# Weight splitting in a two-layer hybrid decoder kernel: half-chunk splits shared by VectorE and GpSimd, against whole-chunk splits on VectorE alone

## The chip, the cores and the metric

The kernel runs on one core of one Trainium2 chip. The time is device microseconds (us) of one execution; before the change it is 1144.73 us, the median of three runs (1144.65 to 1145.38). The engines are called as the profile calls them: PE is the matrix engine (TensorE) and PEld its weight loads, DVE is VectorE, ACT is ScalarE, POOL is GpSimd, and SP is the engine whose queue issues the DMA transfers here. Each engine works through its own list of instructions in order, so an instruction that waits holds all that stand behind it on that engine.

## The reference

Two layers act on x of 256 tokens by 2048 features, in float32. `c` is one vector of 2048, the same for all tokens. In each layer:

```python
shift, scale, gate = jnp.split(silu(c) @ w_ada[l] + b_ada[l], 3, axis=-1)     # w_ada[l]: 2048 x 6144
h = rms_norm(x, norm_w[l]) * (1.0 + scale) + shift
parts = jnp.split(h @ w_in[l], bounds, axis=-1)          # w_in[l]: 2048 x 7704
# three groups of heads read these parts: gated linear attention, gated delta rule, differential attention
y = jnp.concatenate([o_gla, o_gdn, o_diff], axis=-1) @ w_out[l]               # w_out[l]: 2048 x 2048
x = x + gate * y
```

The first line is called the modulation, `h` the modulated input, and the three groups of heads the mixers.

## The kernel before

**Weights.** All large products run on PE with operands of type float32r. To keep float32's accuracy, each operand is split into two parts whose sum is exact, and three products are formed: high by high, high by low and low by high. The modulated input is split into `hh` and `hl` by `modulate`. The weights come from memory in chunks of up to 1024 columns on 128 partitions (512 KB) into one of six buffers `raw`. `weights` (L302) splits each chunk in pieces of 512 or 536 columns: ACT's cast (L316) writes the high part `wh`, and a subtraction of it from `raw` (L319) writes the low part `wl`. Of each seven pieces POOL makes the low part of three and DVE of four. `wh` and `wl` have five buffers of 536 columns each.

**The modulation** has 48 rows of 128 features per layer, in twelve groups of four. Each group needs eight transfers of 1024 columns (`rawa`, from the same six buffers as `raw`); DVE multiplies each by a row of silu(c) and sums along the row in the same instruction (L338), which gives two half sums per feature. When the eighth is done, four or fewer small DVE instructions (L343 to L351) add the halves, the bias, and for the scale the 1 and the norm weight, into `ada`. Groups 0 to 7 give scale and shift for two k tiles each, groups 8 to 11 give the gate. With a k tile's `ada`, `modulate` makes `hn` on DVE (L402), `hh` on ACT (L403) and `hl` on DVE (L404). The function `advance` spreads the groups over the input projection's steps: all twelve of layer 0 and three of layer 1 are done within layer 0.

**Order.** The input projection goes over blocks of output columns and ranges of k tiles (`STEPS`); a block's sums over its range are kept in PSUM (`pt`, `pf`) and are copied out by ACT the first time (L448) and added by DVE later (L450). The mixers are Python generators which are resumed between pieces of the projections, so that their instructions stand between those of the projections on every engine. A scheduler sets each engine's final order by priority and its own estimate; the splits, the modulation's products and the copies from PSUM have a raised priority (`AHEAD`), and the mixers a higher one. The output projection (`py`) follows in three steps and adds into `xr` on DVE (L1200).

**Transfers.** All weights are issued from SP's one queue, `raw` at L308 and `rawa` at L333, in one order. An issue waits there until its buffer has been released by the last reader of what was in it: the low part's subtraction for `raw`, the product for `rawa`.

Of the kernel before, what the change touches and what calls it, by code (L numbers as in the profile page):

```python
# [18 lines left out]
P = 128  # L19
# [3 lines left out]
L = 2  # L23
# [30 lines left out]
# Blocks of columns in the order in which they are computed.  # L54
# [11 lines left out]
# The steps of each layer's input projection: blocks b0..b1-1 over k tiles k0..k1-1. (Layer 0's modulation arrives k tile  # L66
# by k tile, and layer 1's follows the norm.)
# [4 lines left out]
# The k tiles of the output projection's steps: gated linear attention, delta rule, differential attention.  # L72
# [3 lines left out]
def in_chunks(layer, i):  # L76
    """Chunks of w_in for one step: lists of (block, k0, k1) that share one transfer."""
# [23 lines left out]
def _chunk_pieces(chunk):  # L101
    """Sizes of the pieces, of whole k tiles, in which a chunk is split into two parts."""
    out = [0]
    for b, a, z in chunk:
        for _ in range(a, z):
            if out[-1] + _width(b) > 536:
                out.append(0)
            out[-1] += _width(b)
    return out


# Column layout of the packed per-partition parameters.
# [17 lines left out]
def _constants():  # L130
# [6 lines left out]
    # Of each chunk of 64 tokens, its own columns alone.  # L137
# [14 lines left out]
def hybrid_trunk(ctx: ExitStack, tc: tile.TileContext, x, cvec, pos, par, w_ada, w_in, w_out, w_lr, qkn, adt, cst, out):  # L152
# [7 lines left out]
    wsp = ctx.enter_context(tc.tile_pool(name="wsp", bufs=5))  # L160
# [8 lines left out]
    def reg(i, name):  # L169
        """One of the work tiles that the mixers hand on to each other, in the order of the program."""  # L170
        return work.tile([P, 512], F32, name=name, tag=f"R{i}", bufs=1)
# [12 lines left out]
    # The mixers are generators, resumed between pieces of the projections; they yield the tensor engine's time after which  # L184
    # their next step's inputs are expected, or a condition. PSUM banks and work tiles are handed on in this order.
# [905 lines left out]
    for l in range(L):  # L1091
# [132 lines left out]
        if l == 0:  # L1224
            sq = [temp("sqs", T, 1)]
# [81 lines left out]
```

## Time and profile before

| | before |
|---|---|
| median of three runs | 1144.73 us |
| span of the profiled execution, first to last instruction | 1140.7 us |
| busy: PE, DVE, ACT, POOL | 1060.2, 913.4, 613.7, 619.9 us |
| weight pieces split | 620: low part of 354 on DVE, of 266 on POOL |
| products of the modulation (L338) | 192: 184 from `rawa`, 8 from the first tiles `fr` |
| DMA | 273.31 MB, 240 GB/s over the span |

The profile is of one execution. Busy time is the time in which an engine had an instruction running; PE's ends are modelled. In the views by line, a row gives the engine, the operation, the tile written and the tiles read, the shapes and the count, then the busy time and the mean duration of one, and then the idle time just before these instructions with what ended it. The chain of waits is followed back from the last instruction to what released each step. "Issue" in it is time in which an engine waited for nothing that the profile shows.

### The profile page before, as it was taken

How to read it: one execution, taken by the hardware profiler on the slowest of the kernel's cores; microseconds unless marked ns; L12 is line 12 of the kernel's file. 1: busy time of each engine (PE TensorE's matmuls, PEld its weight loads, DVE VectorE, ACT ScalarE, POOL GpSimd, SP SyncE). 2: the span in 40 equal slices, each digit the busy share in tenths (PEclk: the TensorE clock that was granted, in tenths of full speed). 3: DMA queues.
4: the chain of work that ended last, by engine and by line, in shares of the span. 5: the costliest groups of instructions: out<-in, count | busy, mean ns of one | idle time of the engine just before them, and what ended most of it. 6: DMA issues, size and time to landing. Idle time of an engine off the chain costs nothing.

```text
span 1140.7 us, 20595 instructions
## 1 busy us (share of the span) xinstructions
PE 1060.2 (93%) x7398; PEld 927.9 (81%) x7398; DVE 913.4 (80%) x1484; ACT 613.7 (54%) x1367; POOL 619.9 (54%) x550
## 2 busy tenths in 40 slices
PE   4989998889799999999988999998899999999998
PEld 3769876678788886898986877888799877879998
DVE  6899999998999759799788796767656877767853
ACT  4645434445654474666535545476454556557642
POOL 5444444456474586666753554366443666644642
PEclk9999999999999998999998999999899999999999
DMA  9888988888777454666689889785435555667462
GB/s 356 300 291 315 332 292 305 273 290 286 266 258 256 150 166 166 238 206 194 197 283 341 326 313 326 251 310 185 149 99 178 190 183 185 224 219 252 138 201 95
DMA packets 76807, 273.31 MB, mean 240 GB/s; under 512 B 8816, under 2 KB 9888, under 8 KB 76576
## 3 DMA queue, kind: packets, MB, share of 16 engines
q1 hardware_dynamic: 76704, 271.99, 69.8%
q8 instruction: 58, 0.95, 0.3%
q14 instruction: 45, 0.37, 0.1%
HBM read 267.76 MB, written 4.19 MB: 238 GB/s over the span
## 4 chain that ended last, share of the span: by engine, by line
PE 45%; DVE 25%; DMA 11%; issue 9%; POOL 5%; ACT 3%; SPq 0%; DVEq 0%; ACTq 0%; POOLq 0%
PE pt L191 21%; PE py L191 9%; DVE rawa L338 7%; DVE wl L319 7%; DMA rawa<-in_w_ada 7%; PE pf L191 6%; DMA raw<-in_w_in 4%; POOL wl L319 3%; DVE on_gdn L673 2%; PE Z_ps L191 1%; ACT wh L316 1%; PE o_gdn L191 1%; DVE z L450 1%; PE o_gla L191 1%; DVE hn L402 1%
## 5 line engine op out<-in xcount | busy, mean ns | idle before, releaser
L319 POOL TENSOR_TENSOR wl<-raw,wh 128x512 fp32r<-128x512 f32 (+2 forms) x266 | 403.8, 1532 | 355.8 <-ACT wh L316 319.1
L316 ACT CAST wh<-raw 128x512 fp32r<-128x512 f32 (+2 forms) x620 | 367.3, 613 | 311.2 <-PE pt L191 122.6
L338 DVE SCALAR_TENSOR_TENSOR rawa<-rawa,c_row 128x1024 f32<-128x1024 f32 x184 | 262.5, 1431 | 84.3 <-DMA rawa<-in_w_ada 73.0
L319 DVE TENSOR_TENSOR wl<-raw,wh 128x512 fp32r<-128x512 f32 (+2 forms) x354 | 285.5, 821 | 52.1 <-ACT wh L316 50.9
L191 PE MATMUL pt<-wl,hh 128*128 128x512 f32 (+1 forms) x768 | 294.1, 385 | 16.7 <-DVE wl L319 12.7
L191 PE MATMUL pt<-wh,hl 128*128 128x512 f32 (+1 forms) x768 | 289.2, 381 | 1.0 <-DVE hl L404 0.9
L191 PE MATMUL pt<-wh,hh 128*128 128x512 f32 (+1 forms) x768 | 257.4, 383 | 8.5 <-ACT hh L403 6.9
L191 PEld LDWEIGHTS pt<-wl,hh 128*128 128x128 f32 x768 | 146.3, 191 | 52.8 <-DVE wl L319 20.0
L191 PEld LDWEIGHTS pt<-wh,hh 128*128 128x128 f32 x768 | 144.5, 190 | 41.2 <-ACT hh L403 9.1
L191 PEld LDWEIGHTS pt<-wh,hl 128*128 128x128 f32 x768 | 145.8, 190 | 29.6 <-DVE hl L404 2.5
L191 PE MATMUL pf<-hh,wl 128*128 128x256 f32 x512 | 148.8, 292 | 6.4 <-POOL wl L319 4.0
L191 PE MATMUL pf<-hh,wh 128*128 128x256 f32 x512 | 148.2, 290 | 0.0
L191 PE MATMUL pf<-hl,wh 128*128 128x256 f32 x512 | 147.6, 289 | 0.0
L191 PEld LDWEIGHTS pf<-hh,wl 128*128 128x128 f32 x512 | 99.0, 194 | 9.5 <-POOL wl L319 4.9
L191 PEld LDWEIGHTS pf<-hh,wh 128*128 128x128 f32 x512 | 99.4, 194 | 2.3 <-issue 1.2
L191 PEld LDWEIGHTS pf<-hl,wh 128*128 128x128 f32 x512 | 99.1, 194 | 1.1 <-issue 0.7
L191 PE MATMUL py<-ogg,wh 128*128 128x256 f32 x512 | 99.4, 289 | 0.0
L191 PE MATMUL py<-odf,wh 128*128 128x256 f32 x512 | 91.6, 281 | 0.8 <-ACT odf L1044 0.7
L191 PEld LDWEIGHTS py<-ogg,wh 128*128 128x128 f32 x512 | 80.5, 189 | 0.9 <-issue 0.2
L191 PEld LDWEIGHTS py<-odf,wh 128*128 128x128 f32 x512 | 78.4, 188 | 1.5 <-ACT odf L1044 0.9
L191 PE MATMUL py<-odf,wl 128*128 128x256 f32 x256 | 72.0, 282 | 2.6 <-POOL wl L319 1.3
L191 PE MATMUL py<-ogg,wl 128*128 128x256 f32 x256 | 73.1, 287 | 0.0
(279 smaller groups left out, 1416.7 us busy)
## 6 DMA issues: line engine op xcount, KB each, us to landing
raw<-in_w_in SPq DMA_DIRECT2D x224, 512.0 KB, 4.6
rawa<-in_w_ada SPq DMA_DIRECT2D x184, 512.0 KB, 4.7
raw<-in_w_out SPq DMA_DIRECT2D x64, 512.0 KB, 4.2
raw<-in_w_in SPq DMA_DIRECT2D x20, 402.0 KB, 4.1
fr<-in_w_ada SPq DMA_DIRECT2D x8, 512.0 KB, 9.9
xt<-in_x SPq DMA_DIRECT2D x4, 512.0 KB, 5.3
xr<-in_x SPq DMA_DIRECT2D x4, 512.0 KB, 7.8
xs<-xr SPq DMA_DIRECT2D x1, 2048.0 KB, 11.7
```

The lines of the kernel that those rows point to most:

```text
L191: return PE.matmul(o, lhsT=lhsT, rhs=rhs, start=start, stop=stop, **kw)
L316: ACT.copy(wh, r)
L319: e.tensor_tensor(wl, r, wh.bitcast(F32), ALU.subtract)
L338: DVE.scalar_tensor_tensor(raw, raw, 1.0, cb, ALU.mult, ALU.mult, accum_out=sums[:, i:i + 1])
L402: DVE.scalar_tensor_tensor(h, rb, scale, xt[:, i, :], ALU.mult, ALU.mult)
L450: DVE.tensor_tensor(d, src, d, ALU.add)
L673: DVE.scalar_tensor_tensor(yi[:, s:T], src[:, 0:T - s], pcol("conv", w + 3 - s), yi[:, s:T], ALU.mult, ALU.add)
```

## The change

It has three parts.

1. `weights` no longer cuts a chunk into pieces. One ACT cast writes the high part of the whole chunk and one DVE subtraction the low part; POOL has none. `wh` and `wl` now have three buffers of 1024 columns each instead of five of 536. The mixers are still polled after every 536 columns or fewer.
2. The small DVE instructions at the end of a modulation group go. At the start of the program DVE halves the biases and multiplies the norm weights in (three instructions). Then one ACT instruction per feature adds the two half sums, with scale and bias, through its accumulator. There are 96 of these, four per group; each can run when its own feature's two products are done.
3. To make room, `junk` (a discarded output) shrinks from 512 to 256 columns, and `sqs` uses the work tile R9.

```diff
-    wsp = ctx.enter_context(tc.tile_pool(name="wsp", bufs=5))
+    wsp = ctx.enter_context(tc.tile_pool(name="wsp", bufs=3))
...
-    def weights(src, sizes):
-        n = sum(sizes)
-        raw = wraw.tile([P, RAW], F32, name="raw", tag="raw")
+    def weights(src, n):
+        raw = wraw.tile([P, RAW], F32, name="raw", tag="raw")[:, 0:n]
+        wh = wsp.tile([P, RAW], F32R, name="wh", tag="wh")[:, 0:n]
+        wl = wsp.tile([P, RAW], F32R, name="wl", tag="wl")[:, 0:n]
         with tc.high_priority(offset=AHEAD if state["n"] else 0):
-            SP.dma_start(raw[:, 0:n], src)
-        out, off = [], 0
-        for m in sizes:
-            r = raw[:, off:off + m]
-            off += m
-            wh = wsp.tile([P, 536], F32R, name="wh", tag="wh")[:, 0:m]
-            wl = wsp.tile([P, 536], F32R, name="wl", tag="wl")[:, 0:m]
-            with tc.high_priority(offset=AHEAD):
-                ACT.copy(wh, r)
-                state["n"] += 1
-                e = POOL if state["n"] % POOL_WL[1] < POOL_WL[0] else DVE
-                e.tensor_tensor(wl, r, wh.bitcast(F32), ALU.subtract)
-            out.append((wh, wl))
-        return out
+            SP.dma_start(raw, src)
+        with tc.high_priority(offset=AHEAD):
+            ACT.copy(wh, raw)
+            DVE.tensor_tensor(wl, raw, wh.bitcast(F32), ALU.subtract)
+        state["n"] += 1
+        return wh, wl
...
+    DVE.tensor_scalar(pcol("b_ada", 0, 48 * L), pcol("b_ada", 0, 48 * L), 0.5, None, ALU.mult)
+    for l in range(L):
+        DVE.scalar_tensor_tensor(pcol("b_ada", 48 * l + 16, KT), pcol("b_ada", 48 * l + 16, KT), 0.5, pcol("norm", 16 * l, KT),
+                                 ALU.add, ALU.mult)
...
-        s2 = sums.rearrange("p (f u) -> p f u", u=2)
-        s = tiny("ada_s", 4)
-        DVE.tensor_tensor(s, s2[:, :, 0], s2[:, :, 1], ALU.add)
...
+        for f in range(4):
...
+            o, scale = ada[l][:, j, k:k + 1], pcol("norm", 16 * l + k) if j == 0 else 1.0
+            bias = pcol("b_ada", 48 * l + (16, 0, 32)[j] + k)
+            ACT.activation(tiny("ada_j", 2), sums[:, 2 * f:2 * f + 2], AF.Identity, bias=bias, scale=scale, accum_out=o)
...
-            sq = [temp("sqs", T, 1)]
+            sq = [reg(9, "sqs")[:, 0:T]]
```

In the order of instructions, names in brackets are what an instruction waits for: DMAHW is a transfer, the others an engine. Line numbers of the kernel after are lower by 11 to 19 (L301 is the subtraction, L325 the modulation's product, L337 the new sum, L388 to L390 the modulated input).

DVE, layer 0's second modulation group, before: the last product, the small sums and the modulated input stand in one block, and no DVE instruction of it waits for ACT before `hl`.

```order
L338 SCALAR_TENSOR_TENSOR rawa,ada_p<-rawa,c_row 128x1024 [waits DMAHW3_49,DVE_49]
L343 TENSOR_TENSOR ada_s<-ada_p 128x4 [waits DVE_49]
L346 TENSOR_TENSOR ada_s<-ada_s,pt 128x2 [waits DVE_49]
L348 TENSOR_TENSOR ada_144<-ada_s,pt 128x2
L347 SCALAR_TENSOR_TENSOR ada_144<-ada_s,pt 128x2 [waits DVE_49]
L402 SCALAR_TENSOR_TENSOR hn<-rb,ada_144,xt 128x256 [waits DVE_49]
L402 SCALAR_TENSOR_TENSOR hn<-rb,ada_144,xt 128x256
L319 TENSOR_TENSOR wl<-raw,wh 128x512 [waits DMAHW5_49,PE_49,Activation_49]
L338 SCALAR_TENSOR_TENSOR rawa,ada_p<-rawa,c_row 128x1024 [waits DMAHW6_49]
L404 SCALAR_TENSOR_TENSOR hl<-hn,ada_144,hh 128x256 [waits Activation_49] x2
```

The same place after:

```order
L301 TENSOR_TENSOR wl<-raw,wh 128x1024 [waits DMAHW4_49,PE_49,Activation_49]
L388 SCALAR_TENSOR_TENSOR hn<-rb,ada_144,xt 128x256 [waits Activation_49]
L498 CAST posf<-posi 128x2 [waits DMAHW7_49]
L496 TENSOR_SCALAR nexpa<-ea 128x8 [waits Activation_49]
L325 SCALAR_TENSOR_TENSOR rawa,ada_p<-rawa,c_row 128x1024 [waits DMAHW0_49]
L301 TENSOR_TENSOR wl<-raw,wh 128x1024 [waits DVE_49,DMAHW1_49,PE_49,Activation_49]
L325 SCALAR_TENSOR_TENSOR rawa,ada_p<-rawa,c_row 128x1024 [waits DMAHW2_49]
L301 TENSOR_TENSOR wl<-raw,wh 128x1024 [waits DVE_49,DMAHW3_49,PE_49,Activation_49]
L388 SCALAR_TENSOR_TENSOR hn<-rb,ada_144,xt 128x256 [waits Activation_49]
```

The small sums have left DVE, the two `hn` stand apart, each as soon as its own scale is there, and each now waits for ACT.

ACT, the same group, before: `hh` waits for DVE's `hn`, and nothing else of the modulation is on ACT.

```order
L316 CAST wh<-raw 128x512 [waits DMAHW5_49,DVE_49]
L316 CAST wh<-raw 128x512 [waits DVE_49]
L403 ACTIVATE hh<-hn,ada_144 128x256 [waits DVE_49]
L448 COPY z<-pt 128x512 [waits PE_49]
L403 ACTIVATE hh<-hn,ada_144 128x256 [waits DVE_49]
L316 CAST wh<-raw 128x512 [waits DMAHW7_49,Activation_49]
```

The same place after:

```order
L300 CAST wh<-raw 128x1024 [waits DMAHW0_49,DVE_49]
L434 COPY z<-pt 128x512 [waits PE_49]
L337 ACTIVATE ada_j,ada_144<-ada_p,pt 128x2 [waits DVE_49]
L389 ACTIVATE hh<-hn,ada_144 128x256 [waits Activation_49]
L434 COPY z<-pt 128x512 [waits PE_49] x2
L300 CAST wh<-raw 128x1024 [waits DMAHW2_49]
L434 COPY z<-pt 128x512 [waits PE_49] x2
L300 CAST wh<-raw 128x1024 [waits DMAHW4_49]
L337 ACTIVATE ada_j,ada_144<-ada_p,pt 128x2 [waits DVE_49]
```

One cast stands where two stood, and between the casts stand sums that wait for DVE's products.

POOL, in the inversion of layer 0's delta rule (`C`, `Lm` and `E` are its matrices between the tokens of a chunk), before:

```order
L761 TENSOR_TENSOR E<-E,ct 128x512 [waits DVE_49]
L319 TENSOR_TENSOR wl<-raw,wh 128x512 [waits DMAHW7_49,PE_49,Activation_49]
L319 TENSOR_TENSOR wl<-raw,wh 128x512 [waits DVE_49,DMAHW0_49,PE_49,Activation_49]
L319 TENSOR_TENSOR wl<-raw,wh 128x512 [waits DVE_49,PE_49,Activation_49]
L799 TENSOR_TENSOR C<-Lm,ct 128x512 [waits DVE_49,PE_49]
```

The same place after:

```order
L745 TENSOR_TENSOR E<-E,ct 128x512 [waits DVE_49]
L783 TENSOR_TENSOR C<-Lm,ct 128x512 [waits DVE_49,PE_49]
L812 TENSOR_TENSOR on_gdn<-fm 128x512 [waits Activation_49] x2
L783 TENSOR_TENSOR C<-Lm,ct 128x512 [waits PE_49,Pool_49]
L923 TENSOR_TENSOR scr<-aqk,rtab 128x4x64 [waits DVE_49]
```

On POOL the mixers' own instructions are left alone, with no split between them.

## Rows read from the trace of the kernel before

**Rows 1.** The page: busy time of the engines, share of the span, instructions.
```profile
PE 1060.2 (93%) x7398; PEld 927.9 (81%) x7398; DVE 913.4 (80%) x1484; ACT 613.7 (54%) x1367; POOL 619.9 (54%) x550
```

**Rows 2.** Stretches: us; busy (count) of PE, PEld, DVE, ACT, POOL; PE clock; DMA share, GB/s.
```profile
30.00:370.00 340.00, 311.51 (x1961) 265.49 (x1962) 323.92 (x506) 172.08 (x333) 169.60 (x126) 0.98 0.85 290
370.00:1087.00 717.00, 684.71 (x4971) 600.34 (x4966) 546.50 (x905) 408.39 (x982) 416.77 (x396) 0.98 0.64 218
```

**Rows 3.** The chain of waits by line, for 30 to 370 us, then for 370 to 1087.
```profile
by line: DVE rawa L338 16.5%; PE pt L191 15.0%; DVE wl L319 11.7%; issue 9.9%; PE pf L191 7.8%; DMA raw<-in_w_in 5.5%; POOL wl L319 3.7%; DVE on_gdn L673 2.8%; DMA rawa<-in_w_ada 2.5%; DVE z L450 2.3%; DVE av L450 1.9%; DVE hn L402 1.8%; DV
...
by line: PE pt L191 25.4%; DMA rawa<-in_w_ada 10.1%; issue 9.1%; PE py L191 7.8%; DVE wl L319 6.0%; PE pf L191 5.8%; DVE rawa L338 4.0%; DMA raw<-in_w_in 3.1%; POOL wl L319 2.4%; PE o_gdn L191 1.8%; PE Z_ps L191 1.6%; ACT wh L316 1.4%; DVE 
```

**Rows 4.** Timeline about 180 us: POOL, then DVE (start us, us, instruction).
```profile
177.98 5.45 POOL L319 TENSOR_TENSOR wl<-raw,wh 128x512 fp32r<-128x512 f32 x3 [3.77 <-ACT wh L316]
...
180.42 1.25 DVE L343 TENSOR_TENSOR ada_s<-ada_p 128x4 f32<-128x4 f32 x1
...
183.36 0.15 DVE L348 TENSOR_TENSOR ada<-ada_s,pt 128x2 f32<-128x2 f32 x1
183.43 0.68 DVE L450 TENSOR_TENSOR z<-pt,z 128x512 f32<-128x512 f32 x1
```

**Rows 5.** Durations of one instruction on its line: ns min/median/max.
```profile
L338 DVE SCALAR_TENSOR_TENSOR rawa<-rawa,c_row x184: 1206/1221/2366, 29.9 to 1019.7; 128x1024 f32<-128x1024 f32 x184
L402 DVE SCALAR_TENSOR_TENSOR hn<-rb,ada,xt x16: 470/481/1532, 25.6 to 247.8; 128x256 f32<-128x256 f32 x16
```

**Rows 6.** Groups by line and shape, 30 to 370 us, DVE, then POOL.
```profile
L338 DVE SCALAR_TENSOR_TENSOR rawa<-rawa,c_row 128x1024 f32<-128x1024 f32 x88 | 128.1, 1459 | 1.5 <-DMA rawa<-in_w_ada 1.3 <-issue 0.2
L319 DVE TENSOR_TENSOR wl<-raw,wh 128x512 fp32r<-128x512 f32 x102 | 85.7, 858 | 9.4 <-ACT wh L316 9.4
L402 DVE SCALAR_TENSOR_TENSOR hn<-rb,ada,xt 128x256 f32<-128x256 f32 x14 | 11.2, 843 | 0.1
L673 DVE SCALAR_TENSOR_TENSOR on_gdn<-fm,pt,on_gdn 128x253 f32<-128x253 f32 x9 | 7.6, 843 | 0.0
L343 DVE TENSOR_TENSOR ada_s<-ada_p 128x4 f32<-128x4 f32 x11 | 7.5, 678 | 0.1
...
L348 DVE TENSOR_TENSOR ada<-ada_s,pt 128x2 f32<-128x2 f32 x7 | 1.1, 150 | 0.0
...
L319 POOL TENSOR_TENSOR wl<-raw,wh 128x512 fp32r<-128x512 f32 x78 | 126.0, 1631 | 141.0 <-ACT wh L316 132.5 <-DVE rawa L338 8.3 <-POOL wl L319 0.2
```

**Rows 7.** The same stretches, the splits' subtractions alone: busy (count) of DVE, POOL.
```profile
30.00:370.00 340.00, 94.37 (x115) 137.99 (x87) 0.98 0.85 290
370.00:1087.00 717.00, 176.95 (x220) 245.71 (x165) 0.98 0.64 218
```

**Rows 8.** ACT's groups by line and shape over the span.
```profile
L316 ACT CAST wh<-raw 128x512 fp32r<-128x512 f32 x576 | 345.4, 620 | 285.3 <-PE pt L191 105.6 <-DMA raw<-in_w_in 60.7 <-PE py L191 42.7
L563 ACT ACTIVATION_READ_ACCUMULATOR junk<-aqk 128x1 f32 x80 | 15.3, 191 | 0.0
L1082 ACT ACTIVATE sqx<-xt 128x1024 f32<-128x1024 f32 x4 | 4.2, 1057 | 1.8 <-DMA xt<-in_x 1.7
L389 ACT ACTIVATE ms<-ss,eps 128x2 f32<-128x2 f32 x2 | 0.5, 258 | 9.6 <-PE ss L191 9.6
```

**Rows 9.** The splits' line: its DVE durations, and who waited for it (us, times).
```profile
L319 DVE TENSOR_TENSOR wl<-raw,wh x354: 420/683/1834, 27.8 to 1130.7; 128x512 fp32r<-128x512 f32 x165, 128x536 fp32r<-128x536 f32 x7, 128x268 fp32r<-128x268 f32 x5
...
  PEld pt L191: 24.7, 26
...
  PEld pf L191: 8.2, 9
...
  PEld py L191: 3.4, 4
```

**Rows 10.** Waits over the span, then SP's own queue (waiter, releaser, us, times, longest).
```profile
DVE wl L319 <- ACT wh L316: 50.9, 53, 3.3
...
SPq L308 <- DVE rawa L338: 217.2, 105, 5.7
```

More of the change, by code (lines that the diff above doesn't have):

```diff
@@ L98, in _chunk_elems @@
     return sum((z - a) * _width(b) for b, a, z in chunk)
[L101 to L108, printed above, removed]
-    return out
 PAR = {}
@@ L278, in hybrid_trunk @@
     POOL.memset(eps, EPS)
-    junk = const.tile([P, 512], mybir.dt.bfloat16, name="junk")
+    junk = const.tile([P, 256], mybir.dt.bfloat16, name="junk")
     junk_n = [0]
@@ L340, in ada_group @@
                 yield
-        s2 = sums.rearrange("p (f u) -> p f u", u=2)
-        s = tiny("ada_s", 4)
-        DVE.tensor_tensor(s, s2[:, :, 0], s2[:, :, 1], ALU.add)
-        if g < 8:
-            k = 2 * g
-            DVE.tensor_tensor(s[:, 0:2], s[:, 0:2], pcol("b_ada", 48 * l + 16 + k, 2), ALU.add)
-            DVE.scalar_tensor_tensor(ada[l][:, 0, k:k + 2], s[:, 0:2], 1.0, pcol("norm", 16 * l + k, 2), ALU.add, ALU.mult)
-            DVE.tensor_tensor(ada[l][:, 1, k:k + 2], s[:, 2:4], pcol("b_ada", 48 * l + k, 2), ALU.add)
-        else:
-            k = 4 * (g - 8)
-            DVE.tensor_tensor(ada[l][:, 2, k:k + 4], s, pcol("b_ada", 48 * l + 32 + k, 4), ALU.add)
+        for f in range(4):
+            if g < 8:
+                k = 2 * g + f % 2
+                j = 0 if f < 2 else 1
+            else:
+                k = 4 * (g - 8) + f
+                j = 2
+            o, scale = ada[l][:, j, k:k + 1], pcol("norm", 16 * l + k) if j == 0 else 1.0
+            bias = pcol("b_ada", 48 * l + (16, 0, 32)[j] + k)
+            ACT.activation(tiny("ada_j", 2), sums[:, 2 * f:2 * f + 2], AF.Identity, bias=bias, scale=scale, accum_out=o)
         yield
@@ L455, in project @@
             in_off[0] += P * n
-            parts = weights(src, _chunk_pieces(chunk))
-            off = 0
+            wh, wl = weights(src, n)
+            off, polled = 0, 0
             for b, a, z in chunk:
@@ L461, in project @@
                 for k in range(a, z):
-                    if off == parts[0][0].shape[1]:
-                        parts.pop(0)
-                        off = 0
+                    if off + w - polled > 536:
+                        polled = off
                         poll()
-                    wh, wl = parts[0]
                     s = slice(off, off + w)
@@ L560, in head_norm @@
         for h in range(n):
-            a = junk_n[0] % (512 // width) * width
+            a = junk_n[0] % (256 // width) * width
             junk_n[0] += 1
@@ L1060, in out_project @@
             out_off[0] += P * 1024
-            parts = weights(src, [512, 512])
+            wh, wl = weights(src, 1024)
             for i in range(8):
@@ L1065, in out_project @@
                     d = bank("py", "p")[:, 0:T]
-                wh, wl = parts[i // 4]
-                s = slice(128 * (i % 4), 128 * (i % 4) + 128)
+                s = slice(128 * i, 128 * i + 128)
                 mm(d, wh[:, s], ot[k][0], k == 0, False, True)
@@ L1234 @@
 BANKS = {"p": 4, "a": 2, "b": 2}
-POOL_WL = (3, 7)
 PACE = 48
```

1 line of the change is left out of this document (removed).

## The prediction, made before the changed kernel was run

> **What bounds the kernel now.** The page comes first: PE is busy for 93% of the span and DVE for 80%, ACT and POOL for 54% each [rows 1]. A mean over the span hides the stages, so the stretches come next. In A, from 30 to 370 us, where layer 0's projection and its modulation run together, DVE is busy for 323.9 of 340 us, or 95%, and PE for 311.5, which leaves 28.5 idle; the transfers are at 0.85 of their share. In B, from 370 to 1087 us, DVE is at 76% (546.5 of 717) and PE at 95% [rows 2]. Outside A and B I count nothing. The chain of waits then tells what ends last: in A, the DVE lines named in its row make 37.0%, issue 9.9% and POOL's splits 3.7%, together 51%, while PE's two lines make 23%; in B, PE leads with 25.4% for its first line alone, DVE's splits and products make only 10.0%, and POOL's splits 2.4% [rows 3]. So A is where DVE sets the pace, and in B it is one of several.
>
> Why is DVE so full? About 180 us, POOL makes three subtractions in one run, from 177.98 to 183.43. In that time DVE needs 1.25 us for an addition of four columns; the like addition of two columns at the end of POOL's run takes 0.15 us. An addition that reads PSUM takes 0.68 us there [rows 4]. The product of 1024 columns shows the same over the whole span: most take 1.22 us, some up to 2.37 [rows 5]. I read this as DVE being held while POOL works, whenever both of DVE's tensors lie in SBUF.
>
> **The splits in A.** POOL has 87 pieces there and DVE 115 [rows 7]. The pieces of 512 columns are 102 and 78 [rows 6], which is 90 chunks; the other 22, of 268 or 536 columns, make about 8 more. A DVE subtraction of 1024 columns isn't in the trace. The product of as many columns, also with two tensors from SBUF, takes 1.22 us alone [rows 5], and the 512 subtraction 0.68 [rows 9]; instructions in a row overlap by about 0.07 (the one that starts at 183.36 and takes 0.15 is followed at 183.43) [rows 4]. So one end is 1.15 us of DVE per chunk, with nothing holding it; the other is the product's mean in A with POOL as it is, 1.46 - 0.07 = 1.39 [rows 6]. I take 1.15, since most of POOL's work goes. 98 x 1.15 = 112.7 us against 94.4 now [rows 7]: **18.3 us more** on DVE. At 1.39 it would be 41.8, and A's gain below would be gone.
>
> **What DVE gets back in A.** POOL is busy 169.6 us, of which 138.0 are splits [rows 2, 7]; 81% of its work goes. The products have 88 x (1459 - 1221) = 20.9 us of holding [rows 5, 6], and 81% of that is 17.0. The rows of `hn` and of one line of the convolution have 14 x (843 - 481) and 9 x (843 - 481), together 8.3, and 81% is 6.7; the other lines with such excess I leave out as margin. The five small lines from L343 to L351 hold 16.0 us in all, the first 7.5 and the smallest 1.1 [rows 6], and they go to ACT. Sum: 18.3 - 17.0 - 6.7 - 16.0 = **21.4 us less**, or 302.5 instead of 323.9.
>
> If A followed DVE alone, it would take 340 x 302.5 / 323.9 = 317.5 us, 22 less; PE's idle 28.5 us would allow it. If A followed only PE's products and the transfers, it would be 0 less. The chain gives DVE, issue and POOL's splits 51% of A, so I take the middle: **A, 11 us less**.
>
> **ACT in exchange.** A whole-chunk cast should cost what the 1024-column square does, 1.06 us, against two of 0.62. Over the span 288 casts of full chunks replace 576: 288 x (1.24 - 1.06) = 52 us less. The 96 new sums cost at least a small activation with a pointer bias, 0.26, and the accumulator's read, 0.19: 43 us more [rows 8]. ACT stays at 54%; this I count at nothing, since ACT waits for PE to free the split buffers anyway (105.6 us for one line) [rows 8]. The three instructions at the start fall into the wait for the first transfers.
>
> **B.** DVE's load: 385 pieces [rows 7], two to a chunk, make 192 x 1.15 = 221 us instead of 177.0, less whatever holding goes away; even with all 44 added DVE is at 82%. Three terms follow. (1) POOL's splits are 2.4% of the chain, 17.2 us. A piece takes POOL 1.63 [rows 6] and, as half a chunk, DVE 0.575, so a little under two thirds goes: **11 us less**. (2) The holding. Issue is 9.1% of B's chain, 65 us [rows 3], and DVE held by POOL shows there in part; bounds 0 and 65. I take a tenth, because DVE's lines are a tenth of this chain: **6 us less**. The mixers' POOL work, which now waits behind splits, is in this term too. (3) The grain. Where PE waits for a split with nothing ready ahead, a whole chunk takes longer than a half: (1.06 - 0.62) + (1.22 - 0.68) = 0.98 us. PE's loads waited for a low part 26 + 9 + 4 = 39 times [rows 9], and about 17 of those are in B. Bounds: 0 (three buffers of 1024 columns still give two chunks ahead, as four half pieces did) and 17; middle, **8 us more**. In A the grain isn't counted, since there DVE's rate decides and not the delay of one chunk. B together: 11 + 6 - 8 = 9 us less.
>
> **Sum.** 11 + 9 = 20 us, of the profiled execution's 1140.7: 1120.7. The median of the runs lies 4.0 above the span, for what is around it, and nothing there changes: 1144.7 - 20 = **1125 us**. Its own range, from A at 3 and B at 2 less to A at 18 and B at 18 less, is 1109 to 1140.
>
> **The rivals.**
>
> *It gains much more.* DVE is what A waits for throughout, and the holding is a larger part of issue. A gives 22, POOL's splits in B 17, a fifth of issue 13, and the grain costs nothing: 1144.7 - 52 = 1093. For it: the 95%, and small instructions eight times too long. Against it: A's transfers, which run at 290 GB/s already and would have to reach 310.
>
> *The transfers set the pace.* SP waits for buffers which a product releases (217.2 us for L308) [rows 10]. If the loads' own time decides, A's 11 are lost, 1125 + 11 = 1136, and with B's second term 1142; I put it at 1139. For it: 0.85 of the share in A [rows 2]. Against it: SP waits for DVE, which is to have less to do.
>
> *Hand-overs between ACT and DVE eat it.* `hn` now waits for a sum on ACT's queue, which stands behind casts and itself waits for DVE's products. All of DVE's list stands behind that `hn`: splits, products and copies from PSUM, and PE waits for these. The nearest row is DVE's wait for a cast, 50.9 us in 53 times or 0.96 each [rows 10]. 32 tiles at 0.96 are 31 us; those 16 in A count in full (15) and layer 1's 16 by half (8): 1125 + 23 = 1148. If the sums run before their `hn` is reached, as the distance between the two in DVE's new order suggests, it is 0.
>
> *Slower by the grain.* All 39 waits grow by 0.98, and, since a cast also waits for a whole chunk to be freed, each of them comes about twice: 78 x 0.98 = 76 against the 8 counted. In full that is 1125 + 68 = 1193; where half of them are covered, 76 / 2 - 8 = 30 more, 1155, and this is its time. It decides, the kernel getting slower, once the grain costs more than 28 us, or 29 waits of 0.98. For it: PE already waits for low parts 39 times with pieces half as large. Against it: the depth of the buffers is the same. The Trainium skill, Perfetto Trace Analysis, section Optimizing Scalar/DVE Operations, has a rule for each side: larger operations help where the engine is saturated, and breaking them up may help where it isn't but causes bubbles on others. By it A (DVE at 95%) gains and B (76%) loses; no run so far shows the second half, and it is this rival.
>
> **How the numbers follow.** Chances: the forecast 0.53, much more 0.14, transfers 0.11, hand-overs 0.09, grain 0.13. A measurement of this kernel can tell about 0.2%, or 2.3 us, from no change. Faster takes the forecast, the larger gain, and the transfers' case, 0.78; the hand-overs are split, 0.05 within 0.2% and 0.04 slower, and the grain is slower, so that 0.05 are within and 0.17 slower. Range: from 1094, the larger gain's edge, to 1149, the hand-overs' end; the grain's 0.13 and the outer part of the larger gain stay out.
>
> **What would show it.** In A of the new trace DVE's product should have a mean near 1.25 us, its 1024-column subtraction about 1.22, instructions of a few columns that take over 1 us should be nearly gone, and the last piece of layer 0's input projection should end some 10 us earlier. ACT's sums should take about 0.26 + 0.19. A mean of the subtraction over 1.4 would mean that something other than POOL's splits holds DVE. PE's waits for low parts growing in total (36.3 us now) [rows 9], or DVE idle before `hn` waiting for ACT, would make the forecast wrong, and so would a busy DVE in A that falls while A keeps its 340 us.

## The result, and the profile of the kernel after

The changed kernel takes 1104.99 us (median of four runs, 1102.45 to 1107.12) against 1145.06 us for the kernel before (four runs, 1144.65 to 1147.12). The ratio is 0.9634, with an interval from 0.9609 to 0.9659. (The ratios here are those on record with their intervals; they are not quotients of the two medians, which would give 0.9650, and differ from those by up to 0.2%.) It is 40 us faster. The forecast was 20 us faster, 1125; the time lies inside the range, but the gain is twice the one forecast.

The page of the kernel after, busy time and instructions of each engine; it answers to [rows 1].

```profile
PE 1047.0 (95%) x7398; PEld 918.9 (83%) x7398; DVE 888.6 (81%) x1365; ACT 607.2 (55%) x1251; POOL 219.8 (20%) x284
```

POOL's 400 us of splits are gone, and DVE, which took them over, is nevertheless busy for 25 us less than before.

The same two stretches as in [rows 2]: length; busy (count) of PE, PEld, DVE, ACT, POOL; PE clock; DMA share and GB/s.

```profile
30.00:370.00 340.00, 329.52 (x2132) 283.94 (x2131) 323.76 (x491) 192.05 (x379) 39.27 (x46) 0.99 0.87 308
370.00:1087.00 717.00, 692.01 (x5117) 611.61 (x5116) 540.89 (x834) 398.44 (x844) 168.68 (x225) 0.98 0.65 219
```

In A, DVE is exactly as full as before (323.8 us), yet PE makes 2132 matmuls where it made 1961. DVE gets more done in the same time. But it no longer sets the pace alone: PE is now busy for 97% of A, where it was 92%.

The chain of waits by line for these two stretches, against [rows 3].

```profile
by line: PE pt L180 20.9%; PE pf L180 16.1%; DVE rawa L325 10.2%; DVE wl L301 9.9%; issue 9.6%; DMA raw<-in_w_in 6.7%; ACT wh L300 3.2%; DVE aqk L436 2.8%; DVE z L436 2.5%; DVE av L436 1.7%; DMA rawa<-in_w_ada 1.6%; PE o_gla L180 1.3%; DVE 
by line: PE pt L180 19.8%; PE py L180 17.0%; DMA rawa<-in_w_ada 11.5%; PE pf L180 10.4%; issue 8.7%; DVE wl L301 5.0%; DVE rawa L325 3.4%; PE o_gdn L180 1.9%; PE Z_ps L180 1.7%; PE s_ps L180 1.5%; PE o_diff L180 1.3%; PE ropeT_ps L184 1.2%;
```

In A, PE's first two lines now lead with 37.0% (22.8% before), and DVE's products fell from 16.5% to 10.2%. Issue hardly moved, 9.9% to 9.6% in A and 9.1% to 8.7% in B, although the prediction had looked for the holding there.

**The same work, before and after.** A fixed stretch of time holds different work in the two traces, so I compare the stretch in which the same pieces of layer 0 are done: from the first start of the `pf` products to the second. That is 95 to 269 us before and 97 to 251 after. First the stretches before: all instructions, then the splits alone (DVE, POOL).

```profile
95.00:269.00 174.00, 158.88 (x815) 131.41 (x814) 167.45 (x250) 77.45 (x147) 92.24 (x73) 0.99 0.87 302
...
95.00:269.00 174.00, 53.42 (x65) 79.38 (x49) 0.99 0.87 302
```

The same after (splits alone: DVE).

```profile
97.00:251.00 154.00, 152.11 (x799) 129.93 (x798) 147.66 (x216) 75.76 (x131) 13.90 (x24) 0.99 0.94 333
...
97.00:251.00 154.00, 65.39 (x56) 0.99 0.94 333
```

The stretch is 20 us shorter, and so is DVE's busy time (167.45 to 147.66): DVE is at 96% in both, while PE rises from 91% to 99%. The work is the same but for small things at the edges: two `hn` and two `hl` of the stretch before, about 2 us, lie outside the one after. DVE's groups there, before (busy us, mean ns, then idle before them).

```profile
L338 DVE SCALAR_TENSOR_TENSOR rawa<-rawa,c_row 128x1024 f32<-128x1024 f32 x44 | 67.9, 1546 | 1.0 <-DMA rawa<-in_w_ada 0.9
L402 DVE SCALAR_TENSOR_TENSOR hn<-rb,ada,xt 128x256 f32<-128x256 f32 x12 | 8.4, 738 | 0.1
L404 DVE SCALAR_TENSOR_TENSOR hl<-hn,ada,hh 128x256 fp32r<-128x256 f32 x12 | 7.9, 679 | 0.0
L450 DVE TENSOR_TENSOR av<-pt,av 128x512 f32<-128x512 f32 x8 | 5.4, 679 | 0.0
L343 DVE TENSOR_TENSOR ada_s<-ada_p 128x4 f32<-128x4 f32 x5 | 4.1, 818 | 0.0
```

And after.

```profile
L301 DVE TENSOR_TENSOR wl<-raw,wh 128x1024 fp32r<-128x1024 f32 x48 | 58.2, 1214 | 2.0 <-ACT wh L300 1.9
L325 DVE SCALAR_TENSOR_TENSOR rawa<-rawa,c_row 128x1024 f32<-128x1024 f32 x44 | 53.6, 1225 | 2.5 <-DMA rawa<-in_w_ada 2.4
L436 DVE TENSOR_TENSOR av<-pt,av 128x512 f32<-128x512 f32 x8 | 5.1, 676 | 0.0
L388 DVE SCALAR_TENSOR_TENSOR hn<-rb,ada,xt 128x256 f32<-128x256 f32 x10 | 4.7, 474 | 0.0
L390 DVE SCALAR_TENSOR_TENSOR hl<-hn,ada,hh 128x256 fp32r<-128x256 f32 x10 | 4.7, 472 | 0.0
```

The 44 products fell from 1546 to 1225 ns each, 14.3 us in all, and that alone pays for all of POOL's subtractions in the stretch, which cost DVE 65.4 - 53.4 = 12.0 us. `hn` and `hl` fell to their undisturbed durations, and the small sums are gone. The addition that reads PSUM (`av`) takes 679 and 676 ns: it was never held.

**Where the 40 us lie.** The second start of `pf`, and the first `pt` product of layer 1, cut the profiled executions (1140.7 and 1102.2 us) in three.

| us | up to the second `pf` | rest of layer 0 | layer 1 |
|---|---|---|---|
| before | 269.3 | 335.1 | 536.3 |
| after | 251.1 | 330.9 | 520.2 |
| difference | -18.2 | -4.2 | -16.1 |

The prediction's A and B are cut elsewhere (at 370 us), so these parts don't answer to its terms one by one. The middle part hides a gain given back: the second round of `pf` takes 115.8 us before and 96.2 after, and what follows in layer 0 takes 219.3 and 234.7. During that round PE made 1120 matmuls before and makes 817 now; those of the mixers that are missing come behind it.

Part of layer 1's 16 us is PE's clock. Before, the granted clock fell to half, to 1.2 GHz, from 775.5 us for 3.4 us and from 816.4 for 6.8, each time after PE had idled for over 2 us just before (2.4 and 2.2, waiting for a split of POOL's and for a tile of the mixers). In the kernel after it doesn't fall in layer 1 once the `pt` products are under way. By the mean granted clock, 0.987 and 0.995, this is up to 4.4 us of the 16.

**What the prediction asked to look at.** The subtraction's line: durations (min/median/max), and who waited for it, against [rows 9].

```profile
L301 DVE TENSOR_TENSOR wl<-raw,wh x312: 427/1218/2305, 26.7 to 1091.6; 128x1024 fp32r<-128x1024 f32 x144, 128x804 fp32r<-128x804 f32 x12
...
  PEld pt L180: 10.4, 14
...
  PEld pf L180: 4.2, 3
...
  PEld py L180: 1.9, 3
```

PE's loads waited for a low part 20 times and 16.5 us, where it was 39 times and 36.3 us. `hn` after, its durations and what it waited for:

```profile
L388 DVE SCALAR_TENSOR_TENSOR hn<-rb,ada,xt x16: 465/477/481, 25.1 to 219.6; 128x256 f32<-128x256 f32 x16
...
  ACT rb L380: 0.5, 1
```

DVE never stood before an `hn` for one of ACT's new sums. Of DVE's instructions of at most eight columns, 19 took over 1 us before, and none does now. The last `pt` product of layer 0's input projection, which was to end some 10 us earlier, ends 35 us earlier (472.2 to 436.8 us); since mixers' work has moved behind it, 22 of these are left when layer 1 starts. ACT's groups over the span, against [rows 8]:

```profile
L300 ACT CAST wh<-raw 128x1024 fp32r<-128x1024 f32 x288 | 301.2, 1048 | 242.9 <-PE pt L180 96.3 <-PE py L180 45.6 <-issue 36.6
L337 ACT ACTIVATE ada_j<-ada_p,pt 128x2 f32<-128x2 f32 x96 | 31.1, 324 | 80.5 <-DVE rawa L325 72.8 <-DVE fr L325 7.6
L337 ACT ACTIVATION_READ_ACCUMULATOR ada_j<-ada_p,pt 128x1 f32 x96 | 18.0, 188 | 0.0
```

The cast costs what was forecast (1.05 us). The sums cost 49 us instead of 43, and ACT idled 72.8 us in front of them for DVE's products: the wait that the prediction feared exists, but the bound engines didn't feel it.

### The profile page after: what moved, and what is told of

It reads as the page before. It is cut to its first block, busy times and chain, and to the rows that moved or that the text cites. A ratio compares the mean times of both kernels' runs of the same rounds, so it can differ in the third digit from the quotient of the medians.

```text
span 1102.2 us, 19699 instructions
## 1 busy us (share of the span) xinstructions
PE 1047.0 (95%) x7398; PEld 918.9 (83%) x7398; DVE 888.6 (81%) x1365; ACT 607.2 (55%) x1251; POOL 219.8 (20%) x284
## 4 chain that ended last, share of the span: by engine, by line
PE 55%; DVE 18%; DMA 11%; issue 9%; ACT 5%; POOL 2%; SPq 0%; DVEq 0%; ACTq 0%; POOLq 0%
PE pt L180 20%; PE py L180 12%; PE pf L180 12%; DMA rawa<-in_w_ada 8%; DVE wl L301 6%; DVE rawa L325 5%; DMA raw<-in_w_in 2%; ACT wh L300 2%; PE Z_ps L180 1%; PE o_gdn L180 1%; DVE fr L325 1%; PE s_ps L180 1%; DVE aqk L436 1%; DVE z L436 1%; PE o_diff L180 1%
## 5 line engine op out<-in xcount | busy, mean ns | idle before, releaser
L300 ACT CAST wh<-raw 128x1024 fp32r<-128x1024 f32 (+1 forms) x312 | 320.0, 1028 | 272.9 <-PE pt L180 119.4
L301 DVE TENSOR_TENSOR wl<-raw,wh 128x1024 fp32r<-128x1024 f32 (+1 forms) x312 | 384.1, 1236 | 72.2 <-ACT wh L300 68.9
L325 DVE SCALAR_TENSOR_TENSOR rawa<-rawa,c_row 128x1024 f32<-128x1024 f32 x184 | 229.1, 1250 | 74.6 <-DMA rawa<-in_w_ada 74.3
L180 PE MATMUL pt<-wh,hh 128*128 128x512 f32 (+1 forms) x768 | 273.1, 383 | 8.5 <-ACT hh L389 4.3
L180 PE MATMUL pf<-hh,wl 128*128 128x256 f32 x512 | 143.4, 283 | 3.5 <-DVE wl L301 3.5
L180 PE MATMUL pf<-hh,wh 128*128 128x256 f32 x512 | 144.3, 282 | 1.7 <-ACT wh L300 1.6
L180 PE MATMUL pf<-hl,wh 128*128 128x256 f32 x512 | 144.1, 282 | 0.0
L180 PEld LDWEIGHTS pf<-hh,wl 128*128 128x128 f32 x512 | 95.6, 188 | 6.0 <-DVE wl L301 4.2
L180 PEld LDWEIGHTS pf<-hh,wh 128*128 128x128 f32 x512 | 96.1, 188 | 3.1 <-ACT wh L300 1.8
L337 ACT ACTIVATE ada_j<-ada_p,pt 128x2 f32<-128x2 f32 x96 | 31.1, 324 | 80.5 <-DVE rawa L325 72.8
## 6 DMA issues: line engine op xcount, KB each, us to landing
xs<-xr SPq DMA_DIRECT2D x1, 2048.0 KB, 10.2
```

The lines of the kernel that those rows point to most:

```text
L180: return PE.matmul(o, lhsT=lhsT, rhs=rhs, start=start, stop=stop, **kw)
L300: ACT.copy(wh, raw)
L301: DVE.tensor_tensor(wl, raw, wh.bitcast(F32), ALU.subtract)
L325: DVE.scalar_tensor_tensor(raw, raw, 1.0, cb, ALU.mult, ALU.mult, accum_out=sums[:, i:i + 1])
L337: ACT.activation(tiny("ada_j", 2), sums[:, 2 * f:2 * f + 2], AF.Identity, bias=bias, scale=scale, accum_out=o)
```

## The experiments

The theory (H in the expectations) is that POOL's subtractions hold DVE, and that DVE sets layer 0's pace. Four others could explain the same gain or part of it: POOL was slow to release `raw`, so that loads started late (R); POOL's pieces were slow links before PE (Q); whole chunks save or cost something by their grain (G); the new sums bring the gain (S). All medians are of four or more runs, each ratio against runs of the kernel before on the same chip.

| split | old sums (DVE) | new sums (ACT) |
|---|---|---|
| halves, POOL 3 of 7 | 1 (before) | 1.0033 [1.0003, 1.0063] |
| halves, all on DVE | 0.9755 [0.9734, 0.9775] | 0.9699 [0.9683, 0.9714] |
| whole chunks, DVE | 0.9814 [0.9785, 0.9844] | 0.9634 [0.9609, 0.9659] (after) |

And the three parts of the profiled execution (us), cut as above.

| | up to the second `pf` | rest of layer 0 | layer 1 |
|---|---|---|---|
| POOL halves, new sums | 268.3 | 343.5 | 539.0 |
| DVE halves, old sums | 261.4 | 338.0 | 522.5 |
| DVE halves, new sums | 255.3 | 338.2 | 520.2 |
| whole, old sums | 263.3 | 337.7 | 523.5 |
| whole, sums on POOL | 255.0 | 337.9 | 519.1 |
| after, modulation later | 251.7 | 330.7 | 521.1 |
| after with a POOL subtraction | 284.1 | 382.0 | 560.9 |
| after with a POOL memset | 254.3 | 354.4 | 528.7 |
| after, five `raw` | 258.3 | 341.7 | 521.8 |
| after, five `raw`, idle POOL work | 271.5 | 375.4 | 536.9 |

These parts are of one execution each. The first four rows are of one chip, the next four of a second, the last two of the first chip again, later. In these three sets of runs the kernel before takes 1150, 1150 and 1148 us in the median, 3 to 5 more than in the section on the result; a few us between rows of different sets, or against the table of the kernels before and after, mean nothing.

### One part at a time

The halves kept and only POOL taken off, with the old sums:

```diff
-POOL_WL = (3, 7)
+POOL_WL = (0, 7)
```

> The kernel before with all half pieces on DVE, none on GpSimd, and nothing else changed. H: most of the gain comes by this alone, 1112 to 1120, and the modulation's product falls from a mean of 1.43 us to about 1.25. G and S: 1135 or more.

Measured: 1123.04 us, 0.9755. One number, which changes no size and no buffer, brings two thirds of the gain. It shows in the first part (before 269.3) and above all in layer 1 (536.3 to 522.5). DVE's product over the span, before and with this one number changed:

```profile
L338 DVE SCALAR_TENSOR_TENSOR rawa<-rawa,c_row 128x1024 f32<-128x1024 f32 x184 | 262.5, 1431 | 84.3 <-DMA rawa<-in_w_ada 73.0 <-issue 8.7 <-POOL r_d L922 1.8
...
L338 DVE SCALAR_TENSOR_TENSOR rawa<-rawa,c_row 128x1024 f32<-128x1024 f32 x184 | 226.7, 1234 | 68.2 <-DMA rawa<-in_w_ada 67.4
```

The mean falls from 1431 to 1234 ns, as H expected.

The same with the new sums:

```diff
+            ACT.activation(tiny("ada_j", 2), sums[:, 2 * f:2 * f + 2], AF.Identity, bias=bias, scale=scale, accum_out=o)
...
-POOL_WL = (3, 7)
+POOL_WL = (0, 7)
```

> The kernel before with the new sums and with all half pieces on DVE, none on GpSimd; that is the change without whole chunks. H: DVE pays some 300 more starts of 0.08 us, 24 us, a third of it where DVE is full, so 1108 to 1114. G: 1130 or more. S: 1118 or less.

Measured: 1116.41 us, 0.9699. That is 2 us above H's range and within S's; G's 1130 is out. Layer 1 takes 520.2 us, as with whole chunks in the kernel after: as far as runs on two chips can tell, the grain costs and brings nothing there.

Whole chunks with the old sums (the change without its second part):

```diff
-            ACT.activation(tiny("ada_j", 2), sums[:, 2 * f:2 * f + 2], AF.Identity, bias=bias, scale=scale, accum_out=o)
+        DVE.tensor_tensor(s, s2[:, :, 0], s2[:, :, 1], ALU.add)
...
```

> The kernel after with the modulation's sums as they were before (small DVE additions, no ACT sums). Theory H (GpSimd's subtractions held DVE, and the time follows DVE where DVE is full): the holding is gone, and the small additions cost DVE 0.15 us each unheld, some 14 us in all of which a third falls where DVE is full, so about 1110 us. Theory S (the sums on ACT, with hn earlier and finer, bring the most): about 1130. Theory G (whole chunks, with fewer instructions and hand-overs, bring the most): 1108.

Measured: 1127.98 us, 0.9814. S's number came, and H's 1110 was missed by 18 us: with whole chunks, the new sums bring half of the whole gain (0.9814 to 0.9634), and the splits' move off POOL the other half. Here whole chunks are a little worse than halves, while with the new sums they are better.

The new sums alone, with POOL's splits as they were:

```diff
-        DVE.tensor_tensor(s, s2[:, :, 0], s2[:, :, 1], ALU.add)
...
+            ACT.activation(tiny("ada_j", 2), sums[:, 2 * f:2 * f + 2], AF.Identity, bias=bias, scale=scale, accum_out=o)
```

> The kernel before with the new sums on ACT alone; splits in half pieces, three of seven on GpSimd. H: DVE keeps being held; it loses the small additions (31 us with their holding, 16 of it where DVE is full), so 1132 to 1138. S: about 1118. G: 1140.

Measured: 1152.55 us, 1.0033. All three expectations missed. The new sums bring nothing while POOL splits, and 0.6 to 1.8% once it doesn't. Part of the holding seems to move on to the next instructions: DVE's product rises from a mean of 1431 to 1455 ns, its subtraction of 512 columns from 833 to 846; that this eats the whole gain isn't shown. What the sums cost once POOL is off, the whole-chunk kernel with old sums shows. First the group of its first small line in A, then two waits from 30 to 270 us (us, times, longest):

```profile
L325 DVE TENSOR_TENSOR ada_s<-ada_p 128x4 f32<-128x4 f32 x11 | 1.8, 166 | 0.1
```

```profile
DVE rawa L320 <- DMA rawa<-in_w_ada: 10.7, 10, 4.3
PEld pt L180 <- ACT hh L385: 8.7, 3, 5.2
```

With POOL gone, this first of the small lines takes 166 ns instead of the 678 of [rows 6]; the five lines together take 5.7 us in A instead of 16.0. So of the DVE time that the prediction gave to the sums' move, most belongs to the holding. What the old sums still cost is more than their time on DVE, and shows as waits: PE's loads wait 8.7 us for `hh`, and DVE 10.7 us for transfers. In the kernel after, the first wait isn't there, and the second is 3.3 us:

```profile
DVE rawa L325 <- DMA rawa<-in_w_ada: 3.3, 6, 0.9
```

DVE halves, old sums, have 7.4 and 5.6 us of these two waits, and DVE halves, new sums, none and 0.3. That the late `hh` also delays the transfers, by way of split buffers that stay full, is only argued.

### The group's sums on POOL

Whole chunks, and the old group sums, but on POOL: DVE is free of them and ACT has none.

```diff
-        DVE.tensor_tensor(s, s2[:, :, 0], s2[:, :, 1], ALU.add)
+        POOL.tensor_tensor(s, s2[:, :, 0], s2[:, :, 1], ALU.add)
...
```

> The kernel after, with the modulation's small sums per group of four features on GpSimd, which is idle, in place of the sums per feature on ACT. D (the new sums help since DVE is rid of the small additions): 1104 to 1111. F (they help since each feature's sum comes as soon as its own two products are there, so that the modulated input is made earlier and in finer steps): 1122 to 1130, as with the old sums on DVE.

Measured: 1112.73 us, 0.9673 [0.9646, 0.9701]. Most of the new sums' gain (0.9814 to 0.9634) comes without ACT: that DVE is rid of the additions counts, and that each feature is finished by itself is worth at most the 0.4% that is left, where the two intervals still overlap. PE's wait for `hh` is 1.8 us here.

### Work for POOL that reads, or only writes

To hold DVE again without giving any split back, POOL gets work beside the kernel after. It goes on six of seven full chunks, overwrites `raw` when the split is done, and its result is not used. First a subtraction with two inputs from SBUF:

```diff
         DVE.tensor_tensor(wl, raw, wh.bitcast(F32), ALU.subtract)
+            if state["n"] % 7 != 6 and n == 1024:
+                POOL.tensor_tensor(raw[:, 0:512], wh[:, 0:512].bitcast(F32), c_row[:, 0:512], ALU.subtract)
```

> The kernel after, plus an idle GpSimd subtraction (two tensors from SBUF, 128x512) on six of seven full chunks, written over the raw chunk when DVE has read it; its result is not used, and only the next load into that buffer waits for it. This is about the load of subtractions that GpSimd had before. H (holding): DVE's product goes back from a mean of 1.25 us to 1.4 or more, the whole-chunk subtraction likewise, and the kernel to 1128 to 1145 us. Q (what cost time before was waiting for GpSimd's slow pieces and not the holding of DVE): 1104 to 1110, with DVE's durations as in the kernel after or without consequence.

Measured: 1231.66 us, 1.0699 [1.0679, 1.0719]. DVE's split and product, and POOL's new work, over the span:

```profile
L301 DVE TENSOR_TENSOR wl<-raw,wh 128x1024 fp32r<-128x1024 f32 x288 | 413.4, 1444 | 31.9 <-ACT wh L300 31.4
L327 DVE SCALAR_TENSOR_TENSOR rawa<-rawa,c_row 128x1024 f32<-128x1024 f32 x184 | 269.0, 1466 | 78.3 <-DMA rawa<-in_w_ada 74.2 <-POOL sqs L1197 2.6 <-POOL raw L303 1.2
...
L303 POOL TENSOR_TENSOR raw<-wh,c_row 128x512 f32<-128x512 f32 x247 | 421.1, 1709 | 467.1 <-DVE wl L301 442.2 <-issue 9.2 <-DMA raw<-in_w_in 6.2
```

H is exceeded by far: it expected at most 1145. The holding need not be all of this, since POOL's work here also stands in front of the buffers' release. The next run has the release without the reading. It is a memset, which reads nothing:

```diff
+            if state["n"] % 7 != 6 and n == 1024:
+                POOL.memset(raw, 0.0)
```

> The same, but GpSimd only sets the raw chunk to zero (no tensor read, 128x1024). It releases the buffer as late as the run before does. If late release of the raw buffers is what costs, both runs are equally slow; if holding by reads of two tensors costs, this one stays at 1104 to 1110 and DVE's mean durations stay at 1.22 to 1.25 us.

Measured: 1139.29 us, 0.9893 [0.9875, 0.9911]. Neither branch came: DVE's durations stayed, and yet the kernel got slower.

```profile
L301 DVE TENSOR_TENSOR wl<-raw,wh 128x1024 fp32r<-128x1024 f32 x288 | 363.5, 1267 | 54.5 <-ACT wh L300 52.0 <-PE pf L180 1.1
L327 DVE SCALAR_TENSOR_TENSOR rawa<-rawa,c_row 128x1024 f32<-128x1024 f32 x184 | 229.6, 1251 | 92.3 <-DMA rawa<-in_w_ada 90.4 <-POOL raw L303 1.4
```

One of its waits on SP's queue (us, times, longest):

```profile
SPq L322 <- POOL raw L303: 236.8, 93, 17.7
```

The same two lines in the kernel after:

```profile
L301 DVE TENSOR_TENSOR wl<-raw,wh 128x1024 fp32r<-128x1024 f32 x288 | 363.0, 1264 | 65.1 <-ACT wh L300 61.8 <-PE pf L180 2.4
L325 DVE SCALAR_TENSOR_TENSOR rawa<-rawa,c_row 128x1024 f32<-128x1024 f32 x184 | 229.1, 1250 | 74.6 <-DMA rawa<-in_w_ada 74.3
```

Both additions put POOL between the split and the next load into that buffer, so SP's queue now waits for POOL in both; only the one that reads lengthens DVE's instructions (1264 to 1444 and 1250 to 1466, against 1267 and 1251). Holding is thus shown, and that it hangs on POOL's reading. The Trainium skill says this in SBUF — State Buffer, section Who interferes with whom: a DVE instruction with two inputs in SBUF contends with a GpSimd instruction that reads SBUF, and not with one that only writes; the two traces agree, and so does the PSUM reader that stayed at 0.68 us.

What the holding costs shows best up to the second `pf`, where the release is hardly late (POOL's 59 instructions there start 11 us in sum behind DVE's subtraction with the reading, 5 with the memset): DVE is busy for 270.5 of 284.1 us with the reading and for 228.3 of 254.3 with the memset. How the 8% between the two whole runs divide between holding and late release isn't settled; POOL's subtraction takes 1709 ns and the memset 954. The memset also shows a second price: with no holding it still costs 2.6% (0.9634 to 0.9893), and most of that lies in the rest of layer 0 (330.9 to 354.4 us), where the mixers' own instructions on POOL's queue stand in front of the memset that releases the buffer: its 68 memsets there start 67 us in sum after the subtraction they follow.

### Was the late release the cause?

In the kernel before, SP's queue waited for POOL's splits too. If the late release was what cost, another `raw` buffer should win it back. There is room for one only with a split buffer less, so there are two kernels.

```diff
-RAWS = 6
+RAWS = 7
...
-    wsp = ctx.enter_context(tc.tile_pool(name="wsp", bufs=5))
+    wsp = ctx.enter_context(tc.tile_pool(name="wsp", bufs=4))
```

> The kernel before with seven raw buffers in place of six; to make room, the split buffers are four pairs in place of five. To be held against the next run, which has four pairs and six raw buffers. R (in the kernel before, raw buffers come free late since GpSimd's subtractions stand behind the mixers' waiting instructions on its queue, and the loads wait for that): 15 to 30 us faster than the next run. H (it is DVE's being held that costs): within 6 us of it.

> The kernel before with four pairs of split buffers in place of five, six raw buffers as before; the control of the run with seven. The fifth pair hides a piece's delay: 1146 to 1160 us.

Measured: four split buffers alone 1172.54 us, 1.0199 [1.0164, 1.0234]; with the seventh `raw` as well 1180.91, 1.0271 [1.0241, 1.0301]. The fourth pair's 1160 was missed by 12 us, and R's gain didn't come: the seventh buffer doesn't help but costs 0.7%. With four pairs, late release is thus not what holds. For the kernel before itself this is an argument and not proof, since the lost pair brings a limit of its own: ACT's casts wait 164.7 us for PE's `pt` products to free split buffers, where they waited 122.6, and 37.2 us for loads, where they waited 69.2. Loads that start late do cost: the kernel after with one `raw` less loses about 20 us.

```diff
-RAWS = 6
+RAWS = 5
```

> The kernel after with five raw buffers in place of six; the control of the next run, and a measure of what one buffer is worth. If loads that start late set the pace even in the kernel after, 1120 to 1140 us; if not, 1104 to 1112.

Measured: 1125.78 us, 0.9803 [0.9766, 0.9839]. That buffer's room was taken to hold DVE without touching any release: POOL subtracts after each of the 184 products and writes into a tile that nobody reads.

```diff
-RAWS = 6
+RAWS = 5
...
+    idle = const.tile([P, 512], F32, name="idle")
...
+                if raws is None:
+                    POOL.tensor_tensor(idle, c_row[:, 0:512], sums[:, i:i + 1].broadcast_to([P, 512]), ALU.subtract)
```

> The kernel after with five raw buffers, plus a GpSimd subtraction of 512 columns (two tensors from SBUF) behind each of the modulation's 184 products, into a tile that nobody reads. No weight buffer waits for it; it is tied to the product's sum alone. There are 88 of these from 30 to 370 us, as many as GpSimd's pieces there in the kernel before. H: DVE's product goes to a mean of 1.4 us or more, DVE is held some 35 us more in that stretch, and the kernel takes 25 to 45 us more than the run before this one. R: the holding costs under 8 us, since no buffer comes free later.

Measured: 1185.63 us, 1.0308 [1.0277, 1.0339], 60 us more than with five `raw` alone and more than H's 25 to 45; R's 8 are out.

```profile
L302 DVE TENSOR_TENSOR wl<-raw,wh 128x1024 fp32r<-128x1024 f32 x288 | 394.7, 1377 | 42.8 <-ACT wh L301 41.8
...
L328 POOL TENSOR_TENSOR idle<-c_row,ada_p 128x512 f32<-128x512 f32 x184 | 272.1, 1479 | 457.6 <-DVE rawa L326 444.4 <-DVE nb L959 5.6 <-DVE nexpa L499 2.4
```

DVE's product takes 1362 ns in the mean (1256 with five `raw` alone), a little less than H's 1.4 us. DVE is busy for 985.8 us instead of 895.3, and no buffer is released later by the added work itself. But POOL's queue waits 444.4 us for products, and the mixers' instructions wait behind. Only the first part, which is over before most of the mixers' work, is nearly free of that: 258.3 to 271.5 us, 13 us by holding, with 25 us more of DVE's time (228.4 to 253.2); DVE had been at 88% there, so the time follows it only in part. How the other 47 us divide between holding and the mixers' wait isn't settled.

### Was the part given back bound by the modulation?

After layer 0's second `pf` round the kernel gives 15 us back. The modulation's products crowd that round (27 of them between 251 and 350 us). If they push the mixers' work behind it, a plan that puts twelve of them later should change the sum.

```diff
-ADA_BY = {0: ((0, 1), (0, 2), (0, 3), (0, 5), (0, 7), (0, 11), (1, 0), (1, 2)), 1: ((1, 7), (1, 9), (1, 11))}
+ADA_BY = {0: ((0, 1), (0, 2), (0, 3), (0, 5), (0, 7), (0, 9), (0, 11), (1, 2)), 1: ((1, 7), (1, 9), (1, 11))}
```

> The kernel after, with layer 0's last two modulation groups moved from the sixth step of the input projection (where DVE is 96% busy) to the seventh, and layer 1's first three from the seventh step and the output projection to the output projection alone. If DVE's load still sets the pace in the sixth step, its 16 products (19 us of DVE) leave it, and with DVE at 82% in the seventh the kernel gains 5 to 12 us, 1093 to 1100. If the delta rule's own chain sets it by now, 1102 to 1108; if the output projection's products then wait for loads, 1108 to 1115.

Measured: 1110.22 us, 0.9651 [0.9634, 0.9667], not to be told from the kernel after; the first case's 1093 to 1100 did not come. The `pf` round takes 105.7 us instead of 96.2, what follows in layer 0 225.0 instead of 234.7, together 330.7 against 330.9. More of the mixers is done in the round, and the round is longer by just that: the sum is set by something that this plan doesn't touch, and what it is has not been shown.

## Why the prediction was right in its direction and wrong in its size

**What bounds the kernel: right, and not trusted enough.** The reading of [rows 2 to 5], that DVE sets A's pace and that POOL holds it, is what the runs show: POOL off alone 0.9755 with the product back at 1234 ns, and up to the second `pf` 284.1 us with a reading POOL against 254.3 with one that only writes.

**A's terms: right in direction, shifted among themselves.** They gave 21.4 us less for DVE over the 340 us of A. The same work shows 19.8 less (167.45 to 147.66), but within 174 us, with half of A's products (44 of 88). The 65 us of A before it show none (DVE busy for 59.2 us, and for 60.6 after), and behind it the two traces hold no like work, so the sum over all of A is not shown. The subtraction alone was put at 1.15 us a chunk with its overlap; it costs 65.39 / 56 = 1.17 on average, with eight smaller ones among the 56, and 1.20 per 1024 columns. The products' relief was put at 81% of their excess over 1221; in this stretch it was (1546 - 1225) / (1546 - 1221), or 99%. The lines left out as margin were real: `hl` fell from 679 to 472 ns. Against that, the small sums' 16.0 us were counted in full for their move to ACT, while 10.3 of them (16.0 - 5.7) go with POOL already.

**The first step that failed: "I take the middle: A, 11 us less".** Between 0, if A followed PE and the loads, and 22, if it followed DVE alone, the middle came from the chain's 51%. The time followed DVE: in the same work 20.0 us less for 19.8 less of DVE, with DVE at 96% before and after, and 18.2 less by the second `pf`. A share of the chain says who was last in each step, and not by what part the end moves when that engine gets less to do; here the other half of the chain (PE, issue) moved along, since PE had been idle for 15 of the 174 us, and 2 of 154 after.

**The second: the grain, 8 us more.** No run shows a cost of it in layer 1, to which the term belongs. PE's loads waited for low parts for 16.5 us instead of 36.3, and in layer 1 halves and whole chunks take the same 520.2 us with the new sums, and 522.5 and 523.5 with the old. The waits that the term multiplied fell when POOL's splits went, instead of growing; that they were of POOL's slow pieces and the held DVE, and not of a chunk's own delay, is the reading that fits. The page that the prediction weighed, the Trainium skill's Perfetto Trace Analysis, section Optimizing Scalar/DVE Operations, says that smaller pieces may help where the engine isn't saturated but causes bubbles on others; layer 1, with DVE at 72% (376 of 520 us), shows neither gain nor loss by it.

**B's other two terms** were 11 and 6. After the second `pf` the trace is 4.2 + 16.1 = 20.3 us shorter; they sum to 17, though for B alone, which starts at 370. Which of the two holds what isn't shown, nor what of it is PE's clock: issue stayed where it was (9.1% to 8.7%), so it was not the place to look for the holding, which shows in long durations instead. With A at 21.4 and no grain the sum would have been 38, against 38.5 in the profiled executions and 40 in the medians; that it fits so closely is partly luck, since the measured parts are not cut where A and B are. The larger rival had 52: its A (22) and its grain (0) were close, its B too large.

**The other rivals.** Hand-overs from ACT cost nothing: DVE's waits for ACT before `hn` are none. The transfers did not set the pace: in the same work they rose from 302 to 333 GB/s. They are not far from it, as the 20 us for one buffer show. The grain's rival (1155) fell with its term.

**Still open:** why whole chunks lose 0.6% against halves with the old sums and win as much with the new (this across two chips), and which 7 us the kernel after saves in the rest of layer 0 (330.9) against all variants that lack either whole chunks or ACT's sums (338).

## What to carry to other kernels

Where DVE is full and its instructions take longer than their own minimum, look whether GpSimd is reading SBUF at that time, and price the offload with both: what DVE would pay for the work, and what its other two-input instructions get back. Here 44 products got back more (14.3 us) than all the returned work cost (12.0). Where one engine is saturated and the others have room, as here, let the stage's time follow it until the next engine is full, and keep the half for the range; and ask of a wait to be multiplied whether it has the very cause that the change removes.

## What the runs showed of the hardware that was not expected

- The holding lasts to the end of POOL's instruction: a DVE addition of four columns that started at 180.42 us took 1.25 us [rows 4] and ended at 181.67, when POOL's split had ended at 181.65. Where POOL didn't split, it takes 0.17 in the mean.

```profile
179.91 1.74 POOL L319 TENSOR_TENSOR wl<-raw,wh 128x512 fp32r<-128x512 f32 x1
```

- It hangs on POOL's reading: beside 247 memsets of 954 ns each the split stayed at 1267 ns (1264 without).
- An ACT activation of two columns with pointers for scale and bias takes 324 ns in the mean, and its accumulator's read 188: one sum is half a microsecond, where DVE's small addition takes 0.15.
- With four split pairs, a seventh `raw` buffer made the kernel before slower by 0.7%; its fifth pair of split buffers of 536 columns is worth 2%.
